# A hybrid decoder layer on one core: the same instructions of four engines in another written order

## The chip, the core and the metric

The kernel runs on one core of a Trainium2 chip. The metric is the device time of one execution in microseconds (us). The kernel before takes 809.61 us, the median of three runs (809.38, 809.61 and 810.1).

A core has a matrix engine (TensorE, PE in the profile; its weight loads are listed apart as PEld), three engines for elementwise work (VectorE or DVE, ScalarE or ACT, GpSimd or POOL) and SyncE (SP), which here only issues transfers. Each engine runs its own list of instructions in order. Between engines, semaphores make an instruction wait for what it reads or for a buffer that it overwrites.

## The reference

One decoder layer on a sequence of 512 tokens with 1,024 channels. The input projection feeds two mixers side by side: sparse attention with eight heads (compressed, selected and windowed keys; all eight blocks are selected, so the selected branch is a causal attention) and a gated DeltaNet with four heads. The two are projected, merged by gates, projected again and normalised. Then comes a gated MLP with a width-3 convolution, and a second normalisation.

```python
y_a = nsa_attention(nsa_q, cmp_k, cmp_v, slc_k, slc_v, win_k, win_v, nsa_gate, ...) @ w_nsa_out[l]
y_b = gated_deltanet(gdn_qkv, gdn_beta, gdn_decay, gdn_gate, ...) @ w_gdn_out[l]
mix = (jax.nn.sigmoid(gate_a) * y_a + jax.nn.sigmoid(gate_b) * y_b) @ w_o[l]
x = layer_norm(DEEPNORM_ALPHA * x + mix, ln1_g[l], ln1_b[l])
f = conv_ffn(x, ffn_w_up[l], ffn_conv_w[l], ffn_w_down[l])
x = layer_norm(DEEPNORM_ALPHA * x + f, ln2_g[l], ln2_b[l])
```

## The kernel before

Everything is float32. Large products are done as three matmuls of the type fp32r: both operands are split into a high part, a rounded copy, and a low part, the remainder. The three matmuls are high by high, low by high and high by low (L532, L534 and L535 in `product`, L587 to L589 in the first projection, L1328 in the output projection, L1492 in the down projection). Small products of the DeltaNet part are plain float32 and are carried out as two passes, so that the trace has two records for each (L783 and L832 to L908). Transposes are matmuls against an identity (L704, L1113, L1305).

A tile of weights is loaded by SP into a `raw` buffer (three of them), copied to `wh` by ACT (L518, or L520 on another engine) and its remainder is written to `wl` by DVE or POOL (L522); then 24 matmuls of 512 columns read it. The stages by time are: the projection of the rows (to about 20 us); attention and DeltaNet mixed with the remaining input projections (`gps`, to about 325 us); the two output projections and the merge (`pm`, `gps`, to about 413 us); the product with w_o and the first normalisation (`pw`, `pu` L1328, `pt` L1305, to about 450 us); the up-projection with the convolution (`pu` L532 to L535, to about 695 us); the down-projection (`px`, `pz`, `pu` L1492, to 801 us); and the last normalisation on DVE (L1281 to L1293). Some products are replaced by fewer products of sums of blocks. The sums of weight blocks are made in memory by accumulating transfers which POOL issues (`osum` at L551, `wsum` at L561).

In attention a unit of scores is issued at L1080 and L1081 into a bank `aps`, DVE adds the distance term and takes the minimum (L1084), ACT takes the exponential (L1086), and DVE, ACT or POOL apply the factor (L1088, L1094, L1095, L1097). Then PE transposes the result (L1113), ACT and DVE split it (L1116, L1117), and PE multiplies it by the values into `pout` (L1127).

The order is written out by hand. `QUEUES` holds, for each engine, a list of the numbers of its instructions in the order in which the body of the program makes them: "10-12 8-9" says that the instructions 10, 11 and 12 are issued ahead of 8 and 9. `queues` (L385) chains the instructions of each engine in this order and then chains all of them in one row by `TURNS`, a string of engine letters with counts. These chains only fix the order in which instructions are placed. They add no wait on the chip. What an instruction waits for comes from its data and buffers. PE's list has 3,885 entries, DVE's 1,253, ACT's 800, POOL's 169 and SP's 178.

Of the kernel before, what the change touches and what calls it, by code (L numbers as in the profile page):

```python
# [71 lines left out]
def layout(a):  # L72
# [60 lines left out]
    "PE": """0-7 10-12 8-9 16 13 17 14-15 22 18 28 25 29-30 26 23 19 24 20 34 27 37-42 35 21 36 31 52 49-50 46 32 53 33 43 47-48  # L133
44-45 58 51 54 59 61 60 70 62 64-65 71 55 66 76 56-57 63 72-73 77 74 67 75 85-86 68 82 69 78-79 83 87-89 84 90 94
80-81 106 97 91 95 92 96 107 100 93 108-110 101-102 98 111-112 99 113-121 130 122-125 131-134 126-128 135-141 129 142
154 143 155-157 144 158 145 159 146 160-165 147 166-170 148 171 149 172-173 103-104 150 174 151 175-177 182 152-153
183-191 105 192-195 206 196-201 207 202-203 208-209 204 210 205 211-217 234 218-219 178-181 220-224 235 225 236
226-229 237-245 258 246-247 259-261 248 262 249-250 263 251-253 264-266 230-233 254 301 267 302 255-257 268-274
303-306 275-281 307 309 308 310 359-365 282-297 366-367 311-312 368-371 387 313-314 372-373 388 374-375 389-392
376-377 393-394 378-379 395-396 380 397-398 381-382 399-400 298-300 401-408 443-446 409 415-416 410 417-436 447-448  # L140
315 319 316-317 320 318 321 449 322 450 455 437 456 438 457-461 323-326 462-465 327-338 466-468 339-346 469-470
347-354 471-474 355-358 383-385 451 386 475 512 500 476 411 513 501 477 412 452 413-414 453 478 514 502 515 503
516-523 439-441 454 442 524-527 722 528 723-725 529-530 726 504 479-483 506-507 531 727-731 505 484 532-533 485 508
486 732 534 733 535 540 487 734-735 541 736 488-489 737 750-752 490-491 738 753-754 492 542 493 739-740 494 755 741
543 495 544 496 509-511 545-546 497 756-757 498 547-549 499 550 758 559 742 560 743 759-761 551 561-562 564 744 565
745 762 552 763 536-539 563 566 764 590-591 765 580-581 553-554 766 555 567 592-595 568-569 596-598 556 599 557 582
# [190 lines left out]
TURNS = """DA2SPSPSPSPSPSPADSPDPSDP3DPADPASDAPSPDPDP3ASPAPDP4DASP4APDP3ASP2DP5SPAP3APDP2DPASP4APDP4DPAP2DPAP4DP7AP4DP2DP6DP4DP5D  # L337
# [1285 lines left out]
```

## Time and profile before

| | |
|---|---|
| median of 3 runs | 809.61 us |
| the profiled execution | 810.61 us |
| its span, first to last instruction | 808.8 us |
| granted TensorE clock, mean | 0.998 |
| PE idle ahead of its first instruction | 1.0 us |
| span after PE's last matmul (801.0 us) | 7.8 us |

In a page of the profile "busy" is the share of the span in which an engine had an instruction under way. The view of the chain starts from the last instruction and goes back, at each step to what released it or to the instruction ahead of it on its engine. In the timeline the columns are start and length in us, engine, line, operation, output and input, tile sizes and count. In the table by stretch they are the stretch, its length, and then busy time (and number of instructions) of PE, PEld, DVE, ACT and POOL, then PE's clock, the share of DMA time and GB/s. In the groups they are busy us, mean ns of one, then idle time ahead and what ended it.

### The profile page before, as it was taken

What the parts mean: (1) busy time and instruction counts of PE and PEld (TensorE: products, weight loads), DVE (VectorE), ACT (ScalarE), POOL (GpSimd) and SP (SyncE); (2) the same over time, 40 slices, a digit from 0 to 9 for tenths busy, and PEclk for the clock granted to TensorE, in tenths of its full rate; (3) what the DMA queues carried; (4) which work ended last, traced back from release to release, by engine and by line L of the source; (5) the groups of instructions that cost most, each with busy time, mean ns of one, the idle gap of its engine ahead of it and who ended that gap; (6) DMA issues with size and microseconds to landing.
All of it is one profiled execution on the core that took longest, in us unless ns stands there. A gap on an engine that the chain in (4) does not pass through costs nothing.

```text
span 808.8 us, 11746 instructions
## 1 busy us (share of the span) xinstructions
PE 799.8 (99%) x4142; PEld 672.8 (83%) x4142; DVE 601.0 (74%) x1317; ACT 408.3 (50%) x911; POOL 178.8 (22%) x173
## 2 busy tenths in 40 slices
PE   9999999999999999999999999999999999999996
PEld 9888888888888888888888998888888888888885
DVE  5677689989678965486479956676775767877897
ACT  4463678774686764323253333343443444566550
POOL 0345734131265021242200102201111211000001
PEclk9999999999999999999999999999999999999999
DMA  7349550015125049554266933883345772565763
GB/s 286 103 136 347 148 183 27 27 53 123 34 64 148 24 90 187 154 156 128 81 262 192 225 66 123 248 206 101 101 134 192 163 188 66 170 206 181 246 212 131
DMA packets 43259, 119.58 MB, mean 148 GB/s; under 512 B 3264, under 2 KB 4288, under 8 KB 42944
## 3 DMA queue, kind: packets, MB, share of 16 engines
q1 hardware_dynamic: 31136, 87.09, 33.2%
q0 software_dynamic: 11776, 31.46, 16.9%
q8 instruction: 33, 0.54, 0.3%
q10 hardware_dynamic: 288, 0.28, 0.1%
q14 instruction: 26, 0.21, 0.1%
HBM read 116.72 MB, written 33.55 MB: 186 GB/s over the span
## 4 chain that ended last, share of the span: by engine, by line
PE 97%; DVE 2%; issue 0%; ACT 0%; DVEq 0%
PE pu L535 10%; PE pu L532 10%; PE pu L534 10%; PE gps L532 9%; PE gps L535 8%; PE gps L534 8%; PE px L1492 7%; PE pz L1492 4%; PE pw L1328 3%; PE pout L1127 2%; PE aps L1113 2%; PE pu L1328 2%; PE pu L1492 2%; PE pm L532 2%; PE pm L534 2%; PE pm L535 2%
## 5 line engine op out<-in xcount | busy, mean ns | idle before, releaser
L522 DVE TENSOR_TENSOR wl<-raw,wh 128x512 fp32r<-128x512 f32 x146 | 105.0, 724 | 76.3 <-ACT wh L518 31.8
L518 ACT ACTIVATE wh<-raw 128x512 fp32r<-128x512 f32 x126 | 78.8, 629 | 145.2 <-PE pu L534 98.9
L532 PE MATMUL pu<-mh,wh 128*128 128x512 f32 (+1 forms) x384 | 131.4, 373 | 0.0
L534 PE MATMUL pu<-ml,wh 128*128 128x512 f32 (+1 forms) x384 | 130.8, 373 | 0.0
L535 PE MATMUL pu<-mh,wl 128*128 128x512 f32 (+1 forms) x384 | 129.9, 372 | 0.0
L535 PE MATMUL gps<-xh,wl 128*128 128x512 f32 x304 | 118.4, 400 | 0.0
L532 PE MATMUL gps<-xh,wh 128*128 128x512 f32 x304 | 118.1, 400 | 0.1
L534 PE MATMUL gps<-xl,wh 128*128 128x512 f32 x304 | 118.0, 399 | 0.0
L535 PEld LDWEIGHTS pu<-mh,wl 128*128 128x128 f32 x384 | 71.3, 188 | 13.1 <-DVE wl L522 0.2
L534 PEld LDWEIGHTS pu<-ml,wh 128*128 128x128 f32 x384 | 71.5, 188 | 12.7
L532 PEld LDWEIGHTS pu<-mh,wh 128*128 128x128 f32 x384 | 71.2, 188 | 12.4
L1450 DVE SCALAR_TENSOR_TENSOR fa<-pu,fcw,fa 128x511 f32<-128x511 f32 (+1 forms) x88 | 65.1, 745 | 13.6 <-ACT fa L1447 13.0
L1456 POOL TENSOR_TENSOR fth<-fth,fa 128x512 f32<-128x512 f32 x22 | 30.6, 1395 | 196.2 <-DVE fth L1455 125.9
L532 PEld LDWEIGHTS gps<-xh,wh 128*128 128x128 f32 x304 | 57.1, 188 | 10.3 <-issue 0.5
L534 PEld LDWEIGHTS gps<-xl,wh 128*128 128x128 f32 x304 | 57.2, 189 | 9.7
L535 PEld LDWEIGHTS gps<-xh,wl 128*128 128x128 f32 x304 | 57.1, 188 | 9.7
L1427 ACT ACTIVATE wh<-raw 128x512 fp32r<-128x512 f32 x67 | 41.1, 629 | 36.3 <-PE px L1492 8.9
L1428 DVE TENSOR_TENSOR wl<-raw,wh 128x512 fp32r<-128x512 f32 x67 | 45.2, 701 | 15.1 <-ACT wh L1427 14.6
L522 POOL TENSOR_TENSOR wl<-raw,wh 128x512 fp32r<-128x512 f32 x30 | 40.4, 1350 | 17.2 <-ACT wh L518 9.6
L573 POOL TENSOR_TENSOR rs<-rs,minus_half 128x1 f32<-128x1 f32 x8 | 6.7, 840 | 157.3 <-DVE rs L1283 109.1
L1086 ACT ACTIVATE sc<-sc,mn 128x384 f32<-128x384 f32 (+2 forms) x64 | 35.6, 557 | 9.2 <-DVE mn L1084 7.6
L1447 ACT ACTIVATE fa<-pu,fcw 128x512 f32<-128x512 f32 x44 | 29.6, 679 | 19.6 <-PE pu L535 19.4
(372 smaller groups left out, 1730.2 us busy)
## 6 DMA issues: line engine op xcount, KB each, us to landing
raw<-in_up SPq DMA_DIRECT2D x44, 512.0 KB, 3.7
raw<-in_wT SPq DMA_DIRECT2D x40, 512.0 KB, 3.8
wsum<-in_down POOLq DMA_DIRECT2D x6, 2816.0 KB, 21.9
raw<-wsum SPq DMA_DIRECT2D x20, 512.0 KB, 3.8
raw<-in_down SPq DMA_DIRECT2D x15, 512.0 KB, 4.4
osum<-in_wo POOLq DMA_DIRECT2D x6, 1024.0 KB, 10.3
wsum<-wsum POOLq DMA_DIRECT2D x2, 2816.0 KB, 15.4
raw<-in_wm SPq DMA_DIRECT2D x8, 512.0 KB, 4.0
```

Of the source, the lines that this page charges most:

```text
L518: A.activation(wh, r, AF.Copy)
L522: eng.tensor_tensor(wl, r, wh.bitcast(F32), op=OP.subtract)
L532: i = PE.matmul(ps, wh[k], mh_(k), start=(k == 0), stop=False)
L534: PE.matmul(ps, wh[k], ml_(k), start=False, stop=False)
L535: PE.matmul(ps, wl[k], mh_(k), start=False, stop=(k == n - 1))
L1086: A.activation(s[:, i, :n], s[:, i, :n], AF.Exp, scale=-1.0, bias=mn[:, 0, i:i + 1], accum_out=mn[:, 1, i:i + 1])
L1328: PE.matmul(ps[t], a[x](j)[:, ts], w[y][:, j % 2, :], start=fresh and j == 0 and i == 0, stop=j == TT - 1 and i == 2, skip_group_check=True)
L1427: A.activation(hi, raw[:, i], AF.Copy)
L1428: V.tensor_tensor(lo, raw[:, i], hi.bitcast(F32), op=OP.subtract)
L1450: V.scalar_tensor_tensor(acc[:, n:], ps[:, :S - n], w[:, i:i + 1], acc[:, n:], op0=OP.mult, op1=OP.add)
L1456: G.tensor_tensor(th, th, g[1], op=OP.mult)
L1492: m = PE.matmul(ps, a[x][:, j, ts], w[y], start=first and i == 0, stop=last and i == 2, skip_group_check=True)
```

## The change

Only the strings in `QUEUES` and `TURNS` are replaced. The body, the buffers, the engine of each operation and the transfers are the same. The lists of PE, DVE, ACT ("Activation") and POOL are given another order, and `TURNS` is rewritten to match. SP's list stays. Each list holds the same numbers as before. The whole diff is some 500 lines of numbers; below are the beginnings of the lists and the places that are spoken of later.

```diff
 QUEUES = {
-    "PE": """0-7 10-12 8-9 16 13 17 14-15 22 18 28 25 29-30 26 23 19 24 20 34 27 37-42 35 21 36 31 52 49-50 46 32 53 33 43 47-48
...
-814 635 698 869 647 870 636 815 871 699 648-649 637 816 872 700-702 817 703-704 873 638 874-876 639 877-878 705 717
-706-707 718 708 879-883 719-720 884 837-838 721 885-886 709 818 839-842 654 658 655 659 656 660 657 661 853-854
...
-1328-1329 1289 1421 1229 1290 1422 1291-1293 1423 1412 1424 1294-1297 1230-1231 1413 1298 1426 1299 1414 1300 1427
...
-1949-1951 1958 1952 1959 1953-1954 1960-1962 1955 1963-1967 1956 1968 1933-1944 1969-1987 1993-1998 1988-1989 1999
...
+    "PE": """0-7 10-11 8 12 9 13-14 22 16-17 15 18 23 28-29 25-26 24 30 27 34 40 37-38 19-20 35-36 41 39 21 49 42 50 31 52-53 51
...
+837 720 708 881 838 882-883 721 884 709 885-886 839-842 654 658 655 659 656 660 657 661 710 853-854 711 662-665 855
...
+1325-1326 1409-1411 1290 1327 1228 1291 1328 1421 1229 1329 1230 1292 1423-1424 1412 1293 1231 1294 1422 1295-1301
+1426 1302-1303 1427 1413-1417 1304 1378-1379 1418 1380 1428 1425 1429-1431 1442 1305 1381 1443 1382 1419-1420
...
+1946-1948 1957 1949-1950 1958 1951-1953 1959 1954 1960 1955 1961-1967 1956 1968 1933-1944 1969-1986 1993 1987
...
-    "DVE": """0-3 5-6 4 7-10 12 11 13-14 18 15-17 19-20 51-53 22 54 57 23 21 24 58 31 82 32 94 33 28 83 34-35 107 59 36 27 37-38 60
...
-1245-1247 1250 1248-1249 1251-1252""",
+    "DVE": """0-3 5 4 6 8 7 9-12 14 13 15-16 18 20 17 51 19 52-53 28 22 54 23 57 24 21 82 31 58 32-33 94 27 34 26 35-38 59 39 60
...
+1240-1242 1244 1243 1245-1248 1250 1249 1251-1252""",
-    "Activation": """0-3 5 4 7 6 8-12 14 13 15-17 21 24 32 22 27 18 25 28-29 19-20 23 26 31 42 30 34 43 35-37 44 38 45 39 46 40 47 41 62
...
+    "Activation": """0-7 9 8 10-12 14 13 16 15 17 21 24 18 27 22 25 28 23 29 32 19-20 26 30-31 42 34-36 43 37 44 38 45 39 46 40-41 47 62 52
...
-    "Pool": """9-11 13 12 4-5 3 6 14 7 1 15-16 102 17 138 19-22 137 2 8 104 0 26-27 23 32 25 60 33 28 38 29-31 18 42 39 34 101 24 43
...
+    "Pool": """9-13 4-5 14 6-7 1 0 15 102 16 3 17 19 18 20-22 104 2 137 26-27 138 8 23 105 32 25 33 28 36 35 38 29-30 34 31 42 39 43
...
     "SP": """0-7 12 11 13 10 9 8 14-16 18 17 19-67 70 73 71-72 74-75 69 68 76-126 128-155 127 156-157 159 161 163 165-172 164 160
 158 173 162 174-177""",
 }
 
-TURNS = """DA2SPSPSPSPSPSPADSPDPSDP3DPADPASDAPSPDPDP3ASPAPDP4DASP4APDP3ASP2DP5SPAP3APDP2DPASP4APDP4DPAP2DPAP4DP7AP4DP2DP6DP4DP5D
...
+TURNS = """DA2SPSPSPSPSPSPASDPDSPDP4DAPSADAPDSP2DP2DPASP3AP4DASP3ADP4DPASP2DP5DASP3APDP4ASP4AP3ADP3DP2AP3DP4DP5DP2AP7DP3DP2DP9DP3
...
```

More of the change, by code (lines that the diff above doesn't have):

```diff
@@ L138 @@
[L138 to L146, printed above, removed]
-767 584 558 768 570 585 769 571 586 583 795 572-573 600-601 770 574 771-772 575-579 773 587 602 605 796 588 603-604
@@ new lines @@
+2544-2547 2527 2554-2555 2548 2556 2549-2550 2557 2528 2558-2559 2551 2560-2563 2552 2564 2577 2565 2578 2566-2568
+2579-2580 2569 2581-2587 2570-2571 2588-2590 2601 2572-2573 2602-2605 2574 2606-2607 2591 2608 2575 2592 2609 2593
+2576 2610 2594 2611 2595 2612-2613 2596 2614 2625 2597 2615 2626 2598 2627 2616 2628 2599 2629-2632 2617 2600
+2633-2634 2618-2619 2635 2620-2622 2636-2638 2649 2639-2641 2650-2651 2642-2643 2623-2624 2652-2655 2644-2645
+2656-2665 2673 2646-2647 2674-2675 2666 2676 2667 2677 2668-2669 2678 2670 2679 2648 2671 2680-2687 2697 2688
@@ new lines @@
+2816 2841 2831 2842-2848 2832 2849-2853 2833 2854-2855 2834 2856-2857 2835 2858 2836 2865 2859 2866 2837-2839
+2860-2861 2867 2840 2868 2862-2863 2869-2871 2864 2872 2889 2873-2874 2890-2893 2875 2894 2876-2878 2895-2898 2879
+2899 2880 2900 2881-2884 2901 2885 2902-2903 2913 2886 2914 2904 2915 2905 2916-2921 2887 2906 2922 2888 2923-2924
+2907 2925-2926 2908 2927 2937-2940 2909 2928 2941 2910-2911 2942-2945 2912 2946-2947 2929 2948-2950 2930 2951
+2931-2932 2961-2963 2933 2952 2934 2964-2967 2953 2968-2969 2935 2954 2970-2971 2955-2956 2972-2974 2936 2985
@@ new lines @@
+2957-2959 2986 2975 2987-2989 2976 2990-2993 2977 2960 2994 2978-2980 2995 2981 2996-2999 2982 3009-3010 2983
+3000-3001 2984 3011 3002-3006 3012-3014 3007-3008 3015-3020 3033-3034 3021-3022 3035-3040 3023-3024 3041 3025
+3042-3044 3026-3028 3045-3046 3057 3047 3058-3060 3048-3050 3061-3063 3029-3031 3051 3064-3065 3032 3052-3053
+3066-3068 3054 3069-3070 3055 3081 3056 3082-3084 3071 3085-3087 3072 3088-3091 3073 3092 3074-3075 3093 3105
+3076-3077 3106-3108 3094 3109 3095 3078 3110 3096 3111-3114 3079 3097-3098 3115-3116 3080 3099-3102 3129 3103
@@ L382 @@
+P3SPAP2APDP2APDP2DPSP2DP4DP2ADP2AP3ADP3DP3DSPAP2SPDAP3ADP3SPDP5AP3DAP3ADP3DP2DPSAP3DP2APDSP3DPDP2DAP3DP3DP3DSP2ADP3ADP
+DGDP3DPAPDPSP2DP2APDSPAP2DP2DP4SPDPAP2DPAP2DP3DPAPDP2APD2P3SP2ADPDGPAPDP3DP3D2SP2SP2DSPAP2DAPDP3DP2DP7DP3DP4DPD2PGP2D
+P3DP3DSP2SP2DP2SP4DPD6GD3SDS2"""
 PINS = """"""
```

440 lines of the change are left out of this document (216 added, 224 removed), and 3 rows, old and new, of the table QUEUES.

## The prediction

> **What bounds the kernel now.** First the page: busy time by engine, and the shares of the chain that ended last. Then the view of waits, for PE alone.
>
> ```profile
> span 808.8 us, 11746 instructions
> PE 799.8 (99%) x4142; PEld 672.8 (83%) x4142; DVE 601.0 (74%) x1317; ACT 408.3 (50%) x911; POOL 178.8 (22%) x173
> PE 97%; DVE 2%; issue 0%; ACT 0%; DVEq 0%
> ```
> ```profile
> PE gps L606 <- DVE vm L602: 1.0, 1, 1.0
> ```
>
> PE is busy in 99% of the span and makes 97% of the chain. The one wait that the view lists for it is the 1.0 us before its first instruction. But a matmul's record is longer than its turn on the engine, so short waits hide inside "busy". They must be read from the starts. The chain in order of time gives start, length and count of each piece:
>
> ```profile
> 442.70 3.00 PE pw L1328 x13
> 445.69 0.22 PE pt L1305 x2
> 445.91 3.02 PE pw L1328 x13
> 448.93 0.88 PE pt L1305 x8
> 449.80 1.62 PE pw L1328 x7
> 759.18 9.52 PE pz L1492 x42
> 771.87 23.62 PE px L1492 x104
> ```
>
> 23.62/104 is 227 ns for a 512-column matmul in a stretch with nothing between, and 9.52/42 says the same. A kernel whose wide matmuls all stand 227 ns apart has no time on PE that an order could give back. I went through the PE starts for steps clearly longer than the same kind of step elsewhere. After the head these are the ones that a wait explains, in the timeline:
>
> ```profile
> 153.71 0.40 PE L535 MATMUL gps<-xh,wl 128*128 128x512 f32 x1
> 154.18 0.66 PE L1113 MATMUL aps<-ident,sc 128*128 128x128 f32 x4
> ...
> 261.15 0.40 PE L535 MATMUL gps<-xh,wl 128*128 128x512 f32 x1
> 261.48 0.50 PE L1127 MATMUL pout<-ptl,vcat 128*128 128x512 f32 x1
> 261.81 0.39 PE L532 MATMUL gps<-xh,wh 128*128 128x512 f32 x1
> ...
> 390.69 0.39 PE L535 MATMUL gps<-xh,wl 128*128 128x512 f32 x1
> 391.16 0.47 PE L532 MATMUL gps<-xh,wh 128*128 128x512 f32 x1
> ```
>
> From start to start: 0.47 instead of 0.23 at 153.71 (0.24 lost), twice 0.33 at 261.15 and 261.48 (0.21), 0.47 at 390.69 (0.24). Together 0.69 us. In the head there are a few of this kind:
>
> ```profile
> 9.17 0.29 PE L588 MATMUL pb<-wl,xh 128*128 128x288 f32 x1
> 9.39 0.40 PE L589 MATMUL pb<-wh,xl 128*128 128x288 f32 x1
> 9.63 0.30 PE L587 MATMUL pb<-wh,xh 128*128 128x288 f32 x1
> 9.76 0.29 PE L588 MATMUL pb<-wl,xh 128*128 128x288 f32 x1
> ```
>
> A 288-column step is 0.13 (9.63 to 9.76); 9.17 to 9.39 and 9.39 to 9.63 are 0.09 and 0.11 over. With those about 1.0 us of PE's span is waiting that an order could remove. That is 0.12% of the time, and it is the first result: the stock of waits is smaller than the 0.2% (1.6 us) that a measurement of this kernel can tell from no change.
>
> **The change, part by part.** No instruction is added or taken away; four queues get another order and the list of turns follows. To keep the other queue entries in order while turning one list into the other, 1,048 of 3,885 PE entries must move, 380 of 1,253 on DVE, 222 of 800 on ACT, 42 of 169 on POOL; SP's list is the same. No PE entry ends more than 37 places from where it was.
>
> *PE's waits.* The wait at 261.15 is entry 1414 (flip's pout product), which needs the split of the transposes ending with entry 1412. In the old list it stands 12 places behind 1412, in the new one 17. Five more wide matmuls are 1.1 us of cover against 0.1 missing: that step goes, and I count the next with it: minus 0.2. The wait at 390.69 stands behind "1956 1968 1933-1944 1969" in both lists: it stays. The wait at 153.71 is entry 839, a transpose that needs a softmax. Its scores (718) are issued two places earlier, yet what it waits for is DVE:
>
> ```profile
> 145.38 0.60 DVE wl L522
> ...
> 153.41 0.72 ACT sc L1095
> ```
> ```profile
> 120.00:130.00 10.00, 10.00 (x59) 8.80 (x58) 9.99 (x30) 6.86 (x18) 4.92 (x5) 1.00 0.01 2
> 130.00:140.00 10.00, 10.00 (x58) 8.50 (x57) 9.99 (x34) 9.58 (x25) 5.48 (x6) 1.00 0.17 53
> 140.00:150.00 10.00, 10.00 (x57) 8.45 (x55) 9.97 (x45) 7.47 (x21) 0.00 (x0) 1.00 0.17 52
> ```
>
> The first row is a piece of the chain, which runs over DVE from 144 to 153 us and by the second row's ACT step to entry 839; in the table by stretch the fifth column is DVE's busy time, 29.95 of 30 us. While DVE never idles, what counts is how much DVE work stands ahead of the producer. Adding durations in both lists gives the same amount there, so this 0.24 stays too. The same count for every PE entry of that stretch leaves a handful of consumers 0.05 to 0.12 us short that weren't before: plus 0.1 (they don't add up, since one late step delays all that follow), and as ends 0 and the 0.60 of one more DVE instruction. In the head I take no change: minus 0.3 to plus 0.3.
>
> *Runs of plain fp32.* Each matmul that isn't fp32r (transposes, and the two-pass products of the DeltaNet part) breaks the row of 227 ns steps. The old list has 138 such runs, the new one 146. The chain above prices one: after the pair at 445.69 the 13 wide matmuls take 3.02 instead of 13 x 0.227 = 2.95, so 0.07; after the eight at 448.93, 7 take 1.62 instead of 1.59, so 0.03; before them 3.00 is 0.05 over. Eight runs more at 0.05 are plus 0.4 us; the ends are 8 x 0.03 = 0.2 and 8 x 0.07 = 0.6. The runs' own steps are the same instructions and don't change.
>
> *Conversions, loads and sums.* In the stages of weights a tile is copied on ACT and its remainder taken on DVE; loads come through SP, the large sums of weights through POOL.
>
> ```profile
> L522 DVE TENSOR_TENSOR wl<-raw,wh 128x512 fp32r<-128x512 f32 x146 | 105.0, 724 | 76.3 <-ACT wh L518 31.8
> L518 ACT ACTIVATE wh<-raw 128x512 fp32r<-128x512 f32 x126 | 78.8, 629 | 145.2 <-PE pu L534 98.9
> raw<-in_up SPq DMA_DIRECT2D x44, 512.0 KB, 3.7
> wsum<-in_down POOLq DMA_DIRECT2D x6, 2816.0 KB, 21.9
> ```
>
> ACT stands idle 98.9 us before these copies, waiting for PE to give a buffer back: there the work of ACT and DVE hides behind PE, and moving it by a place or two costs nothing until the 0.63 + 0.72 = 1.35 us of one pair no longer fit under the six wide matmuls that take as long. In the new up-projection the shortest place I found misses by under 0.2 us: plus 0.1 (ends 0 and 0.4). On SP nothing moves past anything; its loads go out when a buffer is free, and 3.7 us of landing lie beside 16 wide matmuls. On POOL the first of the two 2.8 MB sums goes from place 16 to 27 and the small osum from 42 to 64; they land 22 us after issue and are read after 380 us, so only their traffic moves. Its cover is what this row shows, where DMA is at 0.77 and PE still has all 40 us; if that failed, one late load would cost up to its 3.7 us:
>
> ```profile
> 60.00:100.00 40.00, 40.00 (x260) 33.58 (x260) 27.00 (x84) 20.36 (x58) 26.04 (x25) 1.00 0.77 250
> ...
> 740.00:780.00 40.00, 40.00 (x178) 33.16 (x177) 34.44 (x53) 23.34 (x36) 0.00 (x0) 1.00 0.71 224
> ```
>
> *The tail.* From PE's last matmul on, the DVE list differs by one pair of neighbours (the two halves of L1289). Both stand ahead of the first L1293, which starts behind the later one in either order: 0.
>
> ```profile
> 795.51 0.70 DVE x L1525
> ...
> 805.20 0.40 DVE x L1293
> ```
>
> Sum: -0.2 + 0.1 + 0.4 + 0.1 = **+0.4 us**. The profiled execution took 810.6 us (its span of 808.8 and 1.8 around it), 1.0 above the median of 809.61; it would become 811.0, and the median **810.0**.
>
> **A page against the trace.** The row of busy times has weight loads at 83%, and the row for 740 to 780 us has 33.16 of 40, also 83%, in a stretch without a gap: a load of 0.19 us under every step of 0.227. By the Trainium skill ("Perfetto Trace Analysis", Identifying the Most-Contended Engine) matmul busy time is a poor measure of headroom, and weight-load share a better one; by that rule 17% of PE would be open to an order. The trace agrees with the first half (the hidden waits above) and not with the second: 83% is what a full stretch shows.
>
> **Rivals.** (1) All waits go and runs cost nothing: 809.6 - 1.0 = 808.6. For it: 261.15 goes. Against it: two of the three named waits stand unchanged. Chance 0.08; still within 0.2%.
>
> (2) PE has room that the starts don't show, as the page's rule would have it. The mixed stages have wide steps a few ns over 227; were the 0.05 us gone from half of the 138 runs, 809.6 - 3.4 = 806.2. Against it: the number of runs rises. Chance 0.07, faster by over 0.2%.
>
> (3) Slower: DVE's full stretch from 118 to 156 us. If the measured handoffs put three more DVE instructions of 0.60 us ahead of what PE needs than the lists' durations say, PE waits 1.8 us there: 809.6 + 0.4 + 1.8 = 811.8. It decides from the second or third instruction; with one it stays inside 0.2%. For it: DVE has nothing left in reserve there, and about 20 of its moved entries lie in it. Against it: the same closeness cost 0.24 us before. Chance 0.18.
>
> (4) A wait long enough to cool PE's clock. The head shows the price: steps of 0.24 us where 0.13 follows later.
>
> ```profile
> 4.68 0.44 PE L588 MATMUL pb<-wl,xh 128*128 128x288 f32 x1
> 4.92 0.49 PE L589 MATMUL pb<-wh,xl 128*128 128x288 f32 x1
> ```
>
> Three us of waiting, the time that the head ran slow, and 1.5 us for as long again at half speed would give 814.5. The longest PE wait behind the start is 0.24 us, so chance 0.03.
> By the Trainium skill ("TensorE: Matmul & The Clock Gate", Why this matters for your kernels) gaps above some 3 us between bursts drop the clock; no stretch here shows such a gap.
>
> (5) The change doesn't do what it says, because the written order isn't what is issued. The old list and the trace agree entry by entry in line numbers on every engine (two PE entries that start within 10 ns aside), so chance 0.02: 809.6.
>
> **How the numbers follow.** The forecast has 0.62. Its own range comes from the ends above: 809.6 - 0.7 - 0.3 + 0.2 = 808.8 with all named waits gone, and 809.6 - 0.2 + 0.6 + 0.6 + 0.4 + 0.3 = 811.3 with every upper end; 0.02 of it lies above 811.2. Faster by over 0.2% (below 808.0): 0.08, rival 2 and a rest of rival 1. Slower (above 811.2): 0.18 + 0.03 + 0.02, less a rest of rival 3 that stays below, 0.22; a late load is counted in rival 3's chance. Within: 0.70. The range from 808.4 to 812.0 leaves out rival 2, rival 4 and the upper part of rival 3, under 0.2 together.
>
> **What would show it.** Right: PE's chain share stays at 97% or so, the step at 261 us is gone, those at entry 839 and at 390 us remain, steps of 227 ns in the last 100 us, and the mixed stages a few tenths longer by more broken rows. Wrong: a new PE step over 1 us anywhere; DVE idle inside 118 to 156 us while PE waits; a load landing late on a copy; or the same count of runs costing less because more of them stand close together, which would take back the +0.4.

## The result, and the profile after

| | before | changed |
|---|---|---|
| median (runs of one comparison) | 809.86 us (4) | 816.71 us (4: 814.81 to 817.89) |
| ratio, 95% interval | | 1.0082 (1.007 to 1.0095) |
| the profiled execution | 810.61 us | 814.81 us |
| its span | 808.8 us | 813.0 us |
| end of PE's last matmul | 801.0 us | 805.4 us |

The changed kernel is slower by 6.9 us. Its page, with the same three lines as before (lines of the source are three higher here: L522 is L525; the kernels below have shifts of their own):

```profile
span 813.0 us, 11762 instructions
PE 799.6 (98%) x4142; PEld 672.4 (83%) x4142; DVE 604.2 (74%) x1317; ACT 411.2 (51%) x911; POOL 176.4 (22%) x173
PE 96%; DVE 3%; issue 0%; ACT 0%; DVEq 0%
```

The shares hardly move. What moved is in the view of waits for PE (engine, line, tile, what it waited for; then us in total, times, longest):

```profile
PE aps L1116 <- DVE ptl L1120: 2.5, 1, 2.5
PE gps L535 <- DVE acc L693: 1.2, 1, 1.2
PE gps L609 <- DVE vm L605: 1.0, 1, 1.0
PE pout L1130 <- DVE ptl L1120: 0.8, 1, 0.8
```

The third row is the old one ahead of the first instruction. The other three weren't in this view before, and each names DVE. The first two are new; the last one is for entry 1414, at which before lost some 0.1 us. The timeline of PE has them as steps from start to start:

```profile
101.96 0.40 PE L538 MATMUL gps<-xh,wl 128*128 128x512 f32 x1
103.54 0.50 PE L535 MATMUL gps<-xh,wh 128*128 128x512 f32 x1 [1.19 <-DVE acc L693]
...
168.02 0.39 PE L535 MATMUL gps<-xh,wh 128*128 128x512 f32 x1
170.95 0.55 PE L1116 MATMUL aps<-ident,sc 128*128 128x128 f32 x3 [2.54 <-DVE ptl L1120]
...
266.07 0.39 PE L1130 MATMUL pout<-pth,vcat 128*128 128x512 f32 x1
267.25 0.50 PE L1130 MATMUL pout<-ptl,vcat 128*128 128x512 f32 x1 [0.79 <-DVE ptl L1120]
```

Steps of 1.58, 2.93 and 1.18 us where a wide matmul takes 0.23: 1.35, 2.70 and 0.95 lost, 5.0 together. Of the small losses of before, those at 153.71 and 261 us (0.45 together) have to be taken off. The head came out 1.0 us shorter. The kernels below with this same order in the head differ by as much there, so that is scatter. 5.0 - 0.45 - 1.0 = 3.55, against 4.2 between the two spans. The other 0.6 lies in smaller steps (one at 40.27 us loses 0.26) and was not followed up. A second trace of the changed kernel (label e7_changed_again) has the same three losses: 1.35, 2.67 and 0.95.

Why is DVE late? Rows of its timeline ahead of the three waits, then that of POOL ahead of the largest (start, length, engine, line, operation, output and input):

```profile
98.41 2.85 DVE L523 CAST wh<-raw 128x512 fp32r<-128x512 f32 x1 [0.18 <-PE gps L537]
...
163.85 0.75 DVE L693 SCALAR_TENSOR_TENSOR acc<-gps,tiny,acc 128x509 f32<-128x509 f32 x1
164.51 5.39 DVE L525 TENSOR_TENSOR wl<-raw,wh 128x512 fp32r<-128x512 f32 x1
169.82 0.47 DVE L1100 TENSOR_SCALAR sc<-sc,mn,gsig 128x384 f32<-128x384 f32 x1
...
264.59 1.34 DVE L819 TENSOR_TENSOR tmp<-lx,xs 128x60 f32<-128x60 f32 x1
```
```profile
160.39 0.63 POOL L1109 CAST vm<-vcb 32x128 fp32r<-32x128 f32 x2
...
162.81 0.72 POOL L554 DMA_DIRECT2D osum<-in_wo  x1
163.56 1.28 POOL L525 TENSOR_TENSOR wl<-raw,wh 128x512 fp32r<-128x512 f32 x1
164.79 1.29 POOL L790 TENSOR_TENSOR at<-at,cst 128x512 f32<-128x512 f32 x1
166.05 1.04 POOL L767 TENSOR_TENSOR grh<-cst,gdh 128x512 fp32r<-128x512 f32 x1
167.06 1.29 POOL L525 TENSOR_TENSOR wl<-raw,wh 128x512 fp32r<-128x512 f32 x1
168.31 1.04 POOL L768 TENSOR_TENSOR grl<-cst,gdl 128x512 fp32r<-128x512 f32 x1
```

A subtraction whose kind took 0.72 us on average in the old kernel stands in the trace for 5.39 us. The profile shows no wait for it and calls DVE busy. It ends at 169.90, when the last of five POOL instructions that stand end to end is over (169.35), not when the one that was running at its start is (164.84). The copy at 98.41 goes the same way, 2.85 us. The small `tmp` at 264.59 stands for 1.34 us beside one POOL subtraction, and for 0.25 in a kernel below (e13) where that one is kept away. In the old kernel the entry of the 5.39 us took this, with POOL at work all the while:

```profile
162.09 0.96 DVE L522 TENSOR_TENSOR wl<-raw,wh 128x512 fp32r<-128x512 f32 x1
```
```profile
161.23 1.27 POOL L522 TENSOR_TENSOR wl<-raw,wh 128x512 fp32r<-128x512 f32 x1
162.47 1.49 POOL L764 TENSOR_TENSOR grh<-cst,gdh 128x512 fp32r<-128x512 f32 x1
163.91 0.28 POOL L1106 CAST vm<-vcb 32x128 fp32r<-32x128 f32 x1
```

### The profile page after: what moved, and what is told of

It reads as the page before. It is cut to its first block, busy times and chain, and to the rows that moved or that the text cites. A ratio compares the mean times of both kernels' runs of the same rounds, so it can differ in the third digit from the quotient of the medians.

```text
span 813.0 us, 11762 instructions
## 1 busy us (share of the span) xinstructions
PE 799.6 (98%) x4142; PEld 672.4 (83%) x4142; DVE 604.2 (74%) x1317; ACT 411.2 (51%) x911; POOL 176.4 (22%) x173
## 4 chain that ended last, share of the span: by engine, by line
PE 96%; DVE 3%; issue 0%; ACT 0%; DVEq 0%
PE pu L538 10%; PE pu L537 10%; PE pu L535 10%; PE gps L538 8%; PE gps L537 8%; PE gps L535 8%; PE px L1495 7%; PE pz L1495 4%; PE pw L1331 3%; PE pout L1130 3%; PE aps L1116 2%; PE pu L1331 2%; PE pu L1495 2%; PE pm L535 2%; PE pm L537 2%; PE pm L538 2%
## 5 line engine op out<-in xcount | busy, mean ns | idle before, releaser
L525 DVE TENSOR_TENSOR wl<-raw,wh 128x512 fp32r<-128x512 f32 x146 | 107.1, 738 | 79.6 <-PE pu L538 36.6
L525 POOL TENSOR_TENSOR wl<-raw,wh 128x512 fp32r<-128x512 f32 x30 | 40.5, 1353 | 16.6 <-ACT wh L521 9.4
```

Of the source, the lines that this page charges most:

```text
L525: eng.tensor_tensor(wl, r, wh.bitcast(F32), op=OP.subtract)
```

## The experiments

A **train** is a row of POOL instructions with no stop between them; a DVE instruction is **held** when it stands in the trace for longer than its own work while POOL runs. The DVE entries are 321 (the copy at 98.41), 431 (the subtraction at 164.51), 406 and 407 (`sc` and `ptl`, next behind it) and 515 (`tmp` at 264.59, two places ahead of the `ptl` that the wait at 267 is for). The POOL entries of the middle train are 65, 45, 55, 67 and 56, of the first 42, 39 and 43. Entry 96 is the one instruction that holds 515. Entry 101 is the issue of the small osum. Entries 34, 83 and 37 are copies into `vm`, of partitions 0 to 31 (34 and 83) and 96 to 127 (37).

The theories: **T1**, a DVE instruction with all operands in SBUF is always held to the end of the train. **T2**, DVE's own new order is late. **T3**, PE or ACT asks for these tiles earlier than they can be had. Later came **T4**, held to the train's end only if it arrives in the last 0.35 us or so of a POOL instruction; **T5**, something else of the full kernel; and **T6**, told below, where the traces led to it. In the list diffs the entries are written singly, the rest of the list is unchanged and `TURNS` is rewritten to match.

### Whose order is it?

The first three change POOL alone. e1 keeps the changed kernel and puts the two subtractions of the train first, then lets POOL begin an instruction behind a DVE instruction at the three places:

```diff
-101 65 45 55 67 56 54
+101 65 67 45 55 56 54
+PINS = """39:321 45:406 96:515"""
+    for p in PINS.split():
+        i, j = (int(n) for n in p.split(":"))
+        tc.add_manual_dep(made["Pool"][i], made["DVE"][j].name, mybir.DependencyInfo(
+            mybir.DependencyClass.Sync, mybir.DependencyReason.DATA), reason="begins behind it")
```

> The changed kernel with three POOL instructions held back: the gate's wl subtract (entry 39) begins behind DVE's wh copy 321, at (entry 45, moved with grh 55 and grl 56 behind wl 67) begins behind DVE's sc 406, and wl 96 begins behind DVE's tmp 515. PE's, ACT's and DVE's orders stay those of the changed kernel. Theory 1 (a DVE instruction with all its operands in SBUF is held up by an unbroken train of POOL instructions, and PE waits for what stands behind it on DVE): DVE 321 falls from 2.85 us to at most 0.9, DVE 431 from 5.39 to about 2.3 (two POOL instructions, not five, are ahead of it), 515 from 1.34 to 0.3; PE's new waits of 1.36, 2.69 and 0.95 us shrink to at most 0.3, 0.4 and 0.3; the time falls by 4 to 6 us to 809.5 to 811.5, a ratio of 1.000 to 1.002 to the kernel before. Theory 2 (DVE's own new order is late, whatever POOL does): the DVE entries keep their places, so the waits and the time stay, 815 to 818. Theory 3 (PE's or ACT's order asks for these tiles earlier than they can be had): 815 to 818 as well.

811.09 us (before 810.02), ratio 1.0014 (1.0005 to 1.0023). All three waits are gone, with PE, ACT and DVE in the new order. Entry 431 takes 2.13 us behind the two subtractions. A wait of 0.73 appears at 339 us, where a POOL subtraction took 2.14. So T2 and T3 fall as the cause of these waits. Some 1.0 us above the kernel before is left.

e2 is the changed kernel with the old POOL list in its first 135 places; e3 is the old kernel with the new POOL list, the same edit the other way round.

```diff
-46 51 62 37 83 63 64 66 89 101 65 45 55 67 56 54
+46 51 62 64 63 37 66 65 55 83 56 36 45 67 49 54
```

> The changed kernel with POOL's list of before in its first 135 places (to about 345 us; behind that POOL's lists agree but for a few neighbours); PE, ACT, DVE and SP keep the orders of the changed kernel. Theory 1: POOL's trains lie where they lay before, DVE's 431 meets at most two POOL instructions in a row and takes under 2 us, and the time is 809 to 812.5; since DVE's order is another, a new meeting of up to 1.5 us is possible. Theories 2 and 3: POOL's order is not the cause, 815 to 818.

813.9 us, 1.0047 (1.0032 to 1.0062): half mended, and 1.4 above the range given. Entry 431 isn't held and 321 takes 0.73, but the wait at 266 stays (0.96) and new ones stand at 67 (1.04), 108 (0.5), 330 (1.1) and 342 us (0.73). The old list isn't good in itself; it fits the old order of the others. These new waits were not followed up.

> The kernel before with POOL's list of the changed kernel alone; PE, ACT, DVE and SP keep the orders of before. Theory 1: the train wl, at, grh, wl, grl now stands at about 161 to 168 us and meets DVE's wl subtract 431 (162.1 us in the profile of before) or sc 406 behind it, so one of them takes over 3 us and PE waits 1 to 3 us at about 165; the time is 811 to 814.5. Theories 2 and 3: POOL's order by itself does nothing, 809.4 to 810.3.

823.79 us, 1.0164 (1.0147 to 1.018): the right side and three times the size. In the timeline, entry 431 and PE:

```profile
166.18 6.56 DVE L521 TENSOR_TENSOR wl<-raw,wh 128x512 fp32r<-128x512 f32 x1
```
```profile
174.32 0.76 PE L531 MATMUL gps<-xh,wh 128*128 128x512 f32 x1 [5.00 <-DVE acc L689]
```

More of the size is in the table by stretch (column after POOL: PE's clock):

```profile
170.00:175.00 5.00, 0.68 (x2) 0.61 (x3) 4.96 (x5) 1.41 (x9) 2.18 (x2) 0.77 0.39 126
175.00:180.00 5.00, 5.00 (x16) 3.98 (x15) 0.77 (x3) 0.23 (x2) 0.00 (x0) 0.54 0.01 3
180.00:185.00 5.00, 5.00 (x32) 4.33 (x31) 3.60 (x13) 3.65 (x15) 0.00 (x0) 1.00 0.00 0
```

After a stop of 5.24 us beyond the usual step (from the last start at 169.05) the clock stands at 0.54 for the next stretch, in which 16 matmuls begin where 5.00/0.227 is 22. In the changed kernel the stop of 2.70 us left it at 1.00. By the Trainium skill ("TensorE: Matmul & The Clock Gate", Why this matters for your kernels) gaps above some 3 us drop the clock; these two agree.

Further steps of this trace lose 1.7 us together at 68 to 70 us, 1.8 at 104.6 and 1.3 at 507.7. The one at 104.6 stands behind a copy (entry 321) held for 3.95 us; the others were not followed up.

e4 tests T2 the other way: in the changed kernel DVE's entry 431 goes behind 406 and 407.

```diff
-411 405 412 431 406 407 446
+411 405 412 406 407 431 446
```

> The changed kernel with one DVE entry moved: the wl subtract 431, which took 5.39 us at 164.51, now stands behind sc 406 and ptl 407, which PE's transposes wait for. POOL's list and the rest stay. Theory 2 (431 stands in front of what PE needs): ptl comes 5 us earlier, the wait of 2.69 us at 168.0 goes, and the time falls by 2.5 us to 812 to 814.5. Theory 1: sc 406 also has its operands in SBUF only, so it takes the place of 431 as the one held up to the end of POOL's train at 169.4; it takes 4.5 to 5.5 us, ptl comes 0.7 us earlier at most, the wait stays at 1.8 to 2.7 us and the time at 814 to 817.5.

814.88 us, 1.0061 (1.0046 to 1.0076). The hold passes to whichever instruction comes:

```profile
165.26 5.03 DVE L1100 TENSOR_SCALAR sc<-sc,mn,gsig 128x384 f32<-128x384 f32 x1
...
170.81 0.67 DVE L525 TENSOR_TENSOR wl<-raw,wh 128x512 fp32r<-128x512 f32 x1
```

PE still waits 1.94 us. DVE's order isn't the cause.

### Do the three waits add up?

```diff
e5:
-101 65 45 55 67 56 54
+101 65 67 45 55 56 54
+PINS = """45:406"""
e6:
+PINS = """39:321 96:515"""
```

> The changed kernel with only the middle place mended: at 45, grh 55 and grl 56 stand behind wl 67 in POOL's list, and 45 begins behind DVE's sc 406. Theory 1, with waits that add up: the wait of 2.69 us at 168.0 goes and those of 1.36 and 0.95 us at 102.0 and 266.1 stay, so the time is about 2.7 us under that of the changed kernel: 812.5 to 814.5. A rival to this (the three waits are one delay handed on from place to place, so that mending one mends those behind it): the wait at 266 goes too, 811 to 812.5.

> The changed kernel with only the outer places mended: wl 39 begins behind DVE's wh copy 321, and wl 96 behind DVE's tmp 515; POOL's list itself is that of the changed kernel, with its train of five. Theory 1, with waits that add up: the waits at 102.0 and 266.1 go (1.36 and 0.95 us), that of 2.69 us stays with DVE's 431 at 5 to 5.6 us; the time is about 2.3 us under that of the changed kernel, 813 to 815.5. The rival of one delay handed on: the wait at 168 shrinks by more than half once the one at 102 is gone, 811 to 812.5.

e5: 813.8 us, 1.0049 (1.0034 to 1.0064); the 2.69 is gone, 1.35 and 0.94 stay, and 0.73 appears at 342 us. e6: 815.26 us, 1.0062 (1.0046 to 1.0079); the outer two are gone, 2.67 stays and entry 431 takes 5.36. In the traces the waits are separate: mending some leaves the others at their size. The medians are 2.9 and 1.45 us under the changed kernel's, where 2.7 and 2.3 were expected; e6's trace has a new wait of 1.0 us at 341. The changed kernel was run again beside them:

> The changed kernel once more, as it is. It was profiled at 814.8 us, while its median is 816.7. Theory 1: DVE's 321, 431 and 515 are held up again (over 2, over 5 and over 1 us), with PE's waits within 0.3 us of 1.36, 2.69 and 0.95; where the time is above 815, the rest is a wait that the profiled run did not have, at the start (a load) or where both engines split weights at about 342 us. Theory 2 or 3: the same three waits, but with DVE's 431 under 2 us in at least this run.

815.16 us, one run; the three waits are back, as said above.

### Is a train enough? Two small kernels

m_lock has no layer in it: DVE's instruction and a train of n POOL subtractions begin behind the same mark.

```python
def trial(n, dk, pk="two", dn=1):
    V.tensor_scalar(go, go, 1.0, None, op0=OP.add)
    G.tensor_copy(fl, go)          # the mark
    for i in range(n):
        pool(pk, i)                # o[i % 2] = a - b
    dve(dk)                        # dv = c - e, begins behind the mark
```

> A kernel that leaves the whole layer out and measures only DVE beside POOL: POOL copies a mark and then runs 0, 1, 2, 3, 5 or 8 subtracts of 128x512 fp32 back to back, and one DVE instruction begins behind the mark. Theory 1 (held to the end of the train): the DVE subtract of two SBUF tiles takes about 0.7 us at 0, then grows by about 1.25 us for each POOL subtract, to about 6.5 at 5 and 10 at 8. Rival (the two engines only share the access): at most 1.4 us however long the train. Rival (it waits only for the POOL instruction that runs when it comes): about 2 us from 1 on. With a train of 5, Theory 1 expects the SBUF copy and the scalar multiply of DVE to be held to its end too, and instructions that read one operand in PSUM to take 0.6 to 0.8 us as without a train. Open: a subtract of 128x16, trains of POOL copies (one operand) and of memsets (none); a lock held by every POOL instruction would hold DVE behind all of them, one that only reads take would not hold it behind memsets. Last trial, the other way round: DVE runs 5 subtracts, POOL's subtract begins behind a mark in front of them; a lock would make POOL's instruction end 1.25 us behind the train, some 4 us from its start.

DVE's subtraction with no train, with one instruction and with eight:

```profile
9.77 0.69 DVE L39 TENSOR_TENSOR dv<-x 128x512 f32<-128x512 f32 x1 [0.29 <-POOL fl L62]
...
11.48 1.81 DVE L39 TENSOR_TENSOR dv<-x 128x512 f32<-128x512 f32 x1 [0.36 <-POOL fl L62]
...
30.45 1.73 DVE L39 TENSOR_TENSOR dv<-x 128x512 f32<-128x512 f32 x1 [0.28 <-POOL fl L62]
```

1.73 us also at 2, 3 and 5: it gets in behind the one that runs, whatever is queued. T1 falls as it was stated; the rival named there, about 2 us, is met. A cast and a scalar product go from 0.43 and 0.49 to 1.46. A subtraction that reads PSUM takes 0.69 with and without a train, and so does the plain one beside memsets; a cast beside memsets takes 1.16, though. The reverse, one POOL subtraction against five of DVE, took 1.63 instead of 1.26: POOL got in behind one, where about 4 was expected.

m_window shifts DVE's arrival in small steps over a whole POOL instruction by a copy from PSUM of 16 to 496 columns ahead of it.

```diff
     for i in range(n):
         pool(pk, i)
+    for w in pre:                          # (512, 16), (512, 48), ... (512, 496)
+        V.tensor_copy(dp[:, :w], ps[:, :w])
     dve(dk)
```

> A kernel that leaves the whole layer out: as in the run before it, POOL runs trains of 5 subtracts (in the last trials 3 and 2) behind a mark; DVE runs copies that read PSUM, of growing width, and then one subtract (or one copy) of SBUF tiles, so that it comes at another point of a POOL instruction in each trial. Theory 4 (the window): DVE's instruction waits for the one POOL instruction that is running, if it comes more than about 0.35 us before that one's end, and takes 0.7 us plus the rest of it; if it comes in the last 0.35 us it is held behind every POOL instruction of the train that follows, 3.5 to 6 us. Theory 1 as first stated (always held to the train's end) has fallen in the run before, where all came early. Rival (Theory 5, something else of the full kernel, such as its traffic or the forms of POOL's instructions, makes the train unbroken): here no arrival is held longer than about 2 us, at whatever point.

Never over 1.80 us: T4 has no window here. The same was asked of the full kernels. e8 moves the DMA issue that sets the arrival behind the train; e9 shifts the old kernel's arrival to just before the end of its first subtraction.

```diff
e8 (changed kernel):
-101 65 45 55 67 56 54
+65 45 55 67 56 101 54
e9 (kernel before):
-64 63 37 66 65 55 83 56 36 45 67 49
+64 63 89 66 65 55 83 56 36 45 67 37 49
```

> The changed kernel with one POOL entry moved: the DMA issue 101 (0.72 us) goes from in front of the train wl, at, grh, wl, grl to behind it. No wait is added; the train of five is whole and starts 0.72 us earlier; DVE's order stays. DVE's wl 431 then comes about 0.85 us before the end of at, not 0.33 before the end of wl. Theory 4 (the window): 431 waits for at only and takes 1.4 to 2.1 us, sc 406 behind it at most 2, the wait of 2.69 us at 168.0 falls to 0 to 0.6, and the time is 812 to 814.5 with the waits at 102 and 266 left. Theory 1 as first stated: 431 is held to the end of the train, at about 168.6 in place of 169.4, it takes over 4 us, the wait stays at 1.6 to 2.1, and the time is 814 to 817.

> The kernel before with two short POOL entries moved, so that its wl 65 ends some 0.2 us earlier: the vm copy 37 (0.29 us and a gap) goes behind the train, the xs copy 89 (0.23 us) comes in front of it. Nothing else is changed. DVE's wl 431 came 0.41 us before the end of POOL's wl 65 there and waited for it alone; now it should come 0.1 to 0.3 us before that end. Theory 4 (the window): it is held behind wl 65, grh 55 and probably vm 83 and grl 56 as well, takes 1.9 to 3.5 us in place of 0.96, ptl is as much later, and the time grows by 0.5 to 2.7 us to 810.5 to 812.7. Rival (the length of what POOL runs decides, not the point at which DVE comes): the two moves change nothing, 809.3 to 810.4.

e8: 815.27 us, 1.0065 (1.0048 to 1.0082); entry 431 still takes 4.65. e9: 810.05 us, 1.0001 (0.9992 to 1.0011); in its timeline 431 came 0.12 us before the end of POOL's subtraction (160.73 + 1.26 = 161.99):

```profile
161.87 0.67 DVE L522 TENSOR_TENSOR wl<-raw,wh 128x512 fp32r<-128x512 f32 x1
```

T4 falls. So a train with no more to it doesn't hold DVE, and the arrival doesn't decide.

### What stands ahead of the train

I then read all traces of the full kernels for DVE instructions between 98 and 167 us that were held past more than one POOL instruction. There were 14. In each a copy into `vm` of 32 partitions stood earlier in the same row without a stop. Those held by one instruction had mostly none ahead. In the old kernel two had one: at 103.1 us DVE came during a DMA issue behind such a copy, and got in as it ended; at 164.41 (`sc`, 1.01 us) only one instruction of the row was left, and POOL then stopped for 0.07 us. **T6**, as it stood ahead of e10: a POOL instruction on 32 of the 128 partitions leaves POOL's partitions out of step, and as long as POOL then runs on, DVE finds no moment between two instructions. The DMA issue was added ahead of e12; that only copies of the first partitions count came out of the small kernels. The orders fit: in the old lists copy 34 stands behind 42 and 39, and 83 behind 55; in the new ones 34 stands ahead of 42, and 83 and the issue 101 ahead of the whole train.

e10 moves the copies behind the trains in the changed kernel; e11 moves one copy ahead of the train in the old one.

```diff
e10 (changed kernel):
-30 34 31 42 39 43 24
+30 31 42 39 43 34 24
-62 37 83 63 64 66 89 101 65 45 55 67 56 54
+62 63 64 66 89 101 65 45 55 67 56 37 83 54
e11 (kernel before):
-64 63 37 66 65 55 83 56 36
+64 63 37 66 83 65 55 56 36
```

> The changed kernel with three short POOL entries moved behind the trains that they stood in front of: the vm copy 34 behind grl 43, the vm copies 37 and 83 behind grl 56. Each copies 32 partitions in about 0.3 us and is needed 33 us or more later. No wait is added, the trains stay unbroken, DVE's order stays. Theory 6 (a POOL instruction on 32 of the 128 partitions puts the partitions out of step, and as long as POOL then runs without a stop a DVE instruction finds no moment between two POOL instructions; without it DVE gets in behind the one that runs): DVE's 321 takes 0.7 to 1.5 us, 431 0.7 to 2.0, PE's waits at 102 and 168 fall to at most 0.6 each, that of 0.95 at 266 stays, and the time is 811 to 813. Theory 1 (always held to the train's end): 321 over 2 us, 431 over 3.5, 814 to 817.

> The kernel before with one short POOL entry moved: the vm copy 83 (32 partitions, 0.28 us), which stood behind grh 55, goes in front of wl 65, so that wl, grh and grl follow it without a stop. Theory 6: DVE's wl 431, which got in behind wl 65 after 0.96 us, is now held behind wl 65, grh 55 and grl 56 and takes 2.5 to 3.5 us; ptl comes 1.5 to 2.5 us later, PE waits 0.5 to 2.5 us for it, and the time is 810.3 to 812.5. Theory 1 and Theory 4 have no place for a 32-partition copy: 431 stays at 0.7 to 2.0 us and the time at 809.3 to 810.4.

e10: 814.09 us, 1.0053 (1.0035 to 1.0071). The wait at 102 us is gone with copy 34. Entry 431 is still held for 4.67, with the DMA issue still ahead: half met. e11: 811.77 us, 1.002 (1.0011 to 1.0029), and in the old kernel, with nothing but this one copy moved, PE now waits 1.82 us at 164.3:

```profile
161.40 3.23 DVE L522 TENSOR_TENSOR wl<-raw,wh 128x512 fp32r<-128x512 f32 x1
```
```profile
160.53 0.29 POOL L1106 CAST vm<-vcb 32x128 fp32r<-32x128 f32 x1
160.79 1.26 POOL L522 TENSOR_TENSOR wl<-raw,wh 128x512 fp32r<-128x512 f32 x1
...
163.03 1.04 POOL L765 TENSOR_TENSOR grl<-cst,gdl 128x512 fp32r<-128x512 f32 x1
```

0.96 became 3.23, to the end of the row of full instructions (164.07; the subtraction ends at 164.63). m_skew does the same with nothing else around it, so T5 falls too: m_lock's trial, with a copy of some partitions ahead of the train and a copy from PSUM ahead of DVE's subtraction.

```python
    for h in head:
        rows = slice(96, 128) if h < 0 else slice(0, h)
        G.tensor_copy(q[rows], a[rows, :128])
    for i in range(n):
        pool(pk, i)
    V.tensor_copy(dp[:, :w], ps[:, :w])    # begins behind the mark
    dve(dk)
```

> A kernel that leaves the whole layer out: as in the runs before it, DVE comes in the middle of the first instruction of a POOL train of subtracts, but now POOL copies 128 columns of 32 partitions (or of 64, of 128, of 32 twice, or of the last 32) right in front of the train. Theory 6: behind the 32-partition copy DVE's subtract of SBUF tiles is held to the end of the train: about 1.5 us at 1, 2.7 at 2, 4 at 3, 6.4 at 5, 10 at 8; with 128 partitions, or without a copy, it takes 1.2 to 1.9 us at 5; 64 and the last 32 act as the first 32. DVE's copy and scalar multiply of an SBUF tile are held as its subtract is, and the subtract that reads PSUM is not (0.7). Rival (Theory 5, something else of the full kernel): at most 2 us in every trial.

Behind a copy of partitions 0 to 31, trains of 1, 2, 3, 5 and 8:

```profile
10.58 1.44 DVE L46 TENSOR_TENSOR dv<-x 128x512 f32<-128x512 f32 x1
...
13.65 2.57 DVE L46 TENSOR_TENSOR dv<-x 128x512 f32<-128x512 f32 x1
...
17.84 3.79 DVE L46 TENSOR_TENSOR dv<-x 128x512 f32<-128x512 f32 x1
...
23.26 6.23 DVE L46 TENSOR_TENSOR dv<-x 128x512 f32<-128x512 f32 x1
...
31.11 9.89 DVE L46 TENSOR_TENSOR dv<-x 128x512 f32<-128x512 f32 x1
...
50.08 1.35 DVE L46 TENSOR_TENSOR dv<-x 128x512 f32<-128x512 f32 x1
...
73.82 1.60 DVE L46 TENSOR_TENSOR dv<-x 128x512 f32<-128x512 f32 x1
```

About 1.2 us more for each instruction of the train. The sixth row is a copy of all 128 partitions ahead of five: 1.35. A copy of 64 holds (6.23), two copies of 32 hold (6.57), DVE's other arrivals are held (6.50 and 6.83), a cast and a scalar product are held too (5.96 each), a subtraction that reads PSUM isn't (0.68). The last row is a copy of partitions 96 to 127, which I expected to hold: 1.60, it doesn't. Which partitions count was an open point.

By the Trainium skill ("SBUF — State Buffer", Who interferes with whom) DVE shares a pair of SBUF ports with GpSimd under an exclusive lock; a DVE instruction with two SBUF inputs contends with a GpSimd instruction that reads SBUF, and the one that comes second blocks for the whole of the first. For the subtraction the kinds agree: beside memsets, and with the PSUM operand, it took 0.69 in m_lock. The extent agrees in m_lock (1.73 behind one of eight) and not here, where 9.89 us go over eight instructions; the measurement decides.

### Which of them counts, and what frees DVE

> The changed kernel with four short POOL entries behind the trains in front of which they stood: the vm copy 34 behind grl 43, and the DMA issue 101 and the vm copies 37 and 83 behind grl 56 (the run with the vm copies alone freed DVE's 321 and left 431 held; the run with the DMA issue alone left both held). No wait is added. Theory 6, widened (a DMA issue on POOL puts it out of step as the 32-partition copies do): 431 gets in behind one POOL instruction and takes 0.7 to 2.0 us, the wait of 1.97 us at 167 falls to at most 0.6, that at 266 (0.95) stays, and the time is 811.3 to 813. Rival (what holds 431 is neither, but the strided copy xs or the run of six instructions as such): 431 stays over 3.5 us and the time at 813 to 815.5.

```diff
e12 (changed kernel): as e10, and the issue 101 behind the train too
-62 37 83 63 64 66 89 101 65 45 55 67 56 54
+62 63 64 66 89 65 45 55 67 56 101 37 83 54
```

811.58 us (before 810.07), 1.002 (1.0011 to 1.003), with no wait added. e8 moved only the issue, e10 only the copies, and each left 431 held for over 4.6 us. With both behind:

```profile
163.26 0.68 DVE L525 TENSOR_TENSOR wl<-raw,wh 128x512 fp32r<-128x512 f32 x1
163.87 1.21 DVE L1100 TENSOR_SCALAR sc<-sc,mn,gsig 128x384 f32<-128x384 f32 x1
```

The waits at 102 and 168 us are gone; the one at 266, behind a single POOL instruction, stays at 0.95. m_skew2 puts other things ahead of a train of five.

```python
for rows in ((0, 16), (0, 32), (32, 64), (64, 96), (96, 128), (0, 96), (64, 128)):
    trial(5, "two", (rows,))
for head in (("issue",), ("strided",), ("issue", "issue")):
    trial(5, "two", head, pre=(512, 512) if len(head) == 2 else (512, 256))
trial(5, "two", (), "chain")              # each reads what the last one wrote
trial(5, "two", ((0, 32),), "chain")
trial(5, "two", ((0, 32), (0, 128)))
trial(5, "two", ((0, 32), "issue"), pre=(512, 512))
```

> A kernel that leaves the whole layer out: DVE's subtract comes in the first or second instruction of a POOL train of five, with other things in front of the train. Theory 6: a copy of partitions 0 to 31 holds it to the train's end (over 5 us; 6.2 in the run before), one of 96 to 127 does not (1.6 there); 0 to 15, 0 to 95 and 64 to 127 show whether it is the first partitions that must lag, as those two say: held for 0 to 15 only if it counts which part lags, not held for 64 to 127. A DMA issue in front of the train holds it too if it is what held 431 in the full kernel (over 3 us), and does not (at most 2) if it is not; the strided copy of 128 partitions does not. A train in which each instruction reads what the last one wrote waits for it between them: there DVE gets in within 2.5 us even behind the copy of partitions 0 to 31; if it is held all the same, such waits are no cure. A copy of all 128 partitions between the 32-partition copy and the train changes nothing: held.

The rows, in the order of the trials that the text speaks of: 0 to 15, 32 to 63, the DMA issue, the chain, and the chain behind 0 to 31:

```profile
10.17 6.32 DVE L50 TENSOR_TENSOR dv<-x 128x512 f32<-128x512 f32 x1
...
25.99 1.59 DVE L50 TENSOR_TENSOR dv<-x 128x512 f32<-128x512 f32 x1
...
66.07 6.30 DVE L50 TENSOR_TENSOR dv<-x 128x512 f32<-128x512 f32 x1
...
95.35 1.12 DVE L50 TENSOR_TENSOR dv<-x 128x512 f32<-128x512 f32 x1
103.17 1.35 DVE L50 TENSOR_TENSOR dv<-x 128x512 f32<-128x512 f32 x1
```

0 to 15, 0 to 31 and 0 to 95 hold (6.32, 6.23, 6.23). 32 to 63, 64 to 95, 96 to 127 and 64 to 127 don't (1.59 to 1.60). A copy with strides over all partitions doesn't either (0.84). A DMA issue holds by itself (6.30). Where each instruction of the train waits for the one before, DVE gets in at once, even behind the copy (1.35); that costs POOL 0.12 us an instruction (1.34 apart instead of 1.22). A copy of all partitions that waits for the small one frees DVE too (1.70, where a hold was expected). A copy of 0 to 31 and an issue together hold (6.13). Two issues gave 0.68, which tells nothing, since DVE came before the train.

By the Trainium skill ("GPSIMD Engine Reference", Instruction dispatch) eight cores of 16 partitions each take every instruction from a queue. The row for 0 to 15 fits cores that run out of step; no run here shows the cores themselves.

e13 is e12 and the pin of the third place; e14 is the changed kernel with all lists as they are, where seven POOL instructions of the two trains wait for the one before them.

```diff
e13:
+PINS = """96:515"""
e14:
+STEPS = """39:42 43:39 65:66 45:65 55:45 67:55 56:67"""
```

> The changed kernel with all three places mended: the four short POOL entries behind the trains, as in the run before, and wl 96 begins behind DVE's tmp 515. Theory 6: the wait of 0.95 us at 262 to 266 goes as well and nothing over 0.6 us is left beside the start, so the time is 0.6 to 1.0 us under that of the run before: 810.5 to 811.1 by its median of 811.6, a ratio to the kernel before of 1.0004 to 1.0013. What then is left over the kernel before (0.3 to 1.0 us) has the eight more runs of plain fp32 matmuls (0.4 us as predicted; the floor of PE's steps is 0.35 to 0.5 us higher in the profiles of all kernels with the changed PE order). Rival (the new order of PE or DVE costs more, hidden so far): 811.3 or more.

> The changed kernel with every list as it is, and seven waits added on POOL alone: wl 39 and grl 43 begin behind the completion of the POOL entry in front of them, and so do wl 65, at 45, grh 55, wl 67 and grl 56. Theory 6 (as in the kernel that measures it alone, where a train whose instructions wait for one another let DVE in behind the first, at 0.12 us for each wait): 321 takes at most 1.5 us and 431 at most 2.0, PE's waits at 102 and 168 fall to at most 0.6 each, that at 266 stays, and the time is 811.3 to 813, as with the entries moved. Theory 1 (held to the train's end, however it is put together): 321 and 431 stay at over 2.8 and 5 us, since waiting for the entry in front takes POOL 0.1 us, and the time at 815 to 818.

e13: 810.07 us (before 809.63), 1.0006 (0.9997 to 1.0015), no longer to be told from the kernel before, with one wait left, the old one of 1.0 us at the start. e14: 811.66 us, 1.0025 (1.0016 to 1.0034), and its timeline, behind the same copies and issue and in the same order as the changed kernel's 5.39:

```profile
163.23 0.88 DVE L531 TENSOR_TENSOR wl<-raw,wh 128x512 fp32r<-128x512 f32 x1
164.03 1.44 DVE L1106 TENSOR_SCALAR sc<-sc,mn,gsig 128x384 f32<-128x384 f32 x1
```

More waiting on POOL made the kernel 5 us faster (816.71 to 811.66, by the medians of two comparisons). With e11, which makes the wait in the old kernel, and e12, which takes it away without a wait, it is shown for both kernels that the copies and the issue ahead of a train are what holds DVE to its end. That POOL's partitions are out of step is T6's picture of it and isn't shown; why the first partitions count stays open.

## Why the prediction was wrong

The forecast was 810.0 us in a range to 812.0; 816.7 came. The list of signs named the right one: "a new PE step over 1 us anywhere".

**The step that failed** is this one: "On POOL the first of the two 2.8 MB sums goes from place 16 to 27 and the small osum from 42 to 64; they land 22 us after issue and are read after 380 us, so only their traffic moves." It counts the issue as a transfer alone. The issue, entry 101, is also an instruction of POOL, now ahead of the longest train. The rest of POOL's new order has no term in the sum, so the copies 34 and 83 aren't spoken of either. Copy 34 lets the first train hold DVE for 2.85 us, and 83 or the issue, each enough by itself (e8 and e10), lets the middle one hold it for 5.39; PE lost 1.35 and 2.70 us by that. (The 22 us of landing in that step is the row of `wsum`; the row of `osum` has 10.3. Nothing hangs on it.) Beside it failed "Adding durations in both lists gives the same amount there": durations on DVE were taken as its own, though a POOL instruction lengthens them. Rows of before showed this much: a subtraction of the same kind stood there for 0.69 us at 145.30, with POOL idle, and for 0.96 at 162.09, with POOL at work (the 0.60 at 145.38 in the prediction is a piece of the chain, not the whole instruction). The holds past several instructions, however, weren't to be had from rows of before at that length; the third wait, behind one POOL instruction, was of a known kind and its place could have been looked for.

By its other steps:

- The wait at 261.15 "goes": this failed too. It is the wait of entry 1414, and 1414 is what waits 0.95 us at 267.25. The cover on PE did grow, by somewhat more than the 1.1 counted: from entry 1412 to 1414, the waits left out, it is 3.45 us where it was 2.19. But DVE's `ptl` comes behind the `tmp` that POOL held for 1.34 us. With that hold gone (e1, e6, e13) the wait is gone.
- The wait at 390.69 "stays": it does, 0.25 at 395.22.
- The wait at 153.71 "stays too": it went.
- The 0.1 for DVE's full stretch, 118 to 156 us: no new wait there. The trouble lay at 98 and at 164 us, on both sides of it.
- Runs of plain fp32, +0.4: the count (138 to 146) is right, the price isn't shown. The usual step of each kind, summed over all of PE's steps, comes out between 0.5 us less and 0.6 more than before, depending on how kinds are told apart. e13, with the three waits gone, is 0.44 above the kernel before, within the noise.
- Conversions, +0.1: nothing seen. The tail, 0: right.
- Rival 3 (slower, through DVE, chance 0.18) had the side, not the place or the mechanism: DVE had no more work, it was kept from working. Rival 4, the clock, didn't come here; e3 showed it at a stop of 5.24 us. Rivals 1, 2 and 5 fell. That the forecast lay on the slow side at all is luck: what put it there, the +0.4, isn't what made the kernel slower. PE's weight-load share is 83% in the slower kernel too, and no order tried was faster than before.

What isn't settled: the runs without a profile are some 2 us above the two traced ones of the changed kernel, and what they wait for was not seen. The traces of e4 and e6 have a further wait of 1.0 us near 342 us, and those of e1, e2 and e5 one of 0.7 there, where DVE and POOL both split weights; that it comes and goes between runs of one kernel is a guess.

## What to carry to other kernels

When instructions of POOL and DVE are put in another order, look at each train of POOL beside what DVE must deliver in that time, and keep short copies of the first partitions and DMA issues out of the place just ahead of it; behind the train they added no wait here. Where they can't move, a wait of each POOL instruction for the one before it costs 0.12 us and lets DVE in. Don't add up DVE durations as if they were its own: an instruction that stands much longer than others of its form while POOL runs a train may be held, and the engine's busy share and waits won't say so. A kernel with 1 us of waits in all can win little from an order and can lose much more.

## What the runs showed of the hardware

- DVE's subtraction, cast and scalar product from SBUF wait for one POOL instruction that reads SBUF (1.73 us instead of 0.69 for the subtraction), even with eight queued. The cast also waited beside memsets (1.16 instead of 0.43).
- Behind a POOL copy that includes partitions 0 to 15 and not all, or behind a DMA issue, they wait for the whole train: 1.44, 2.57, 3.79, 6.23 and 9.89 us at 1, 2, 3, 5 and 8. Copies that begin at partition 32, 64 or 96 don't do this.
- A wait between POOL's instructions undoes it (1.35 us).
- An operand in PSUM in place of one of the two in SBUF keeps DVE's subtraction free of it (0.68 us).
